# Cutting the w_up matmuls of a hybrid decoder layer into parts of other widths and column orders

## The chip, the cores and the metric

The kernel runs on one core of one Trainium2 chip. The metric is the device time of one execution in microseconds (us). A core has five engines that run side by side: PE (TensorE, matrix multiplication), DVE (VectorE), ACT (ScalarE), POOL (GpSimd) and SP (SyncE, which here only issues DMAs). The profile shows two rows for PE: PE is the streaming of a matmul's columns, PEld is the loading of its stationary operand, the "weights" of that one instruction, which may overlap the matmul before it.

## What is computed

One decoder layer over a sequence of 256 tokens with model width 2048. Attention comes first, and then the part that the change touches: a gated MLP whose up-projection is followed by a causal convolution of width 3 over time.

```python
D_MODEL = 2048
SEQ = 256
D_FF = 5632
...
        x = x + rmsnorm(mix, post_mix_g[l])
        h = rmsnorm(x, pre_ffn_g[l])
        u = causal_dwconv(h @ w_up[l], conv_w[l], conv_b[l])
        gate, val = jnp.split(u, 2, axis=-1)
        y = (jax.nn.gelu(gate, approximate=True) * val) @ w_down[l]
        x = x + rmsnorm(y, post_ffn_g[l])
```

All of it is float32. `w_up` is 2048 x 11264, so `h @ w_up` has 44 blocks of 256 output columns: 22 for the gate and 22 for the value.

## The kernel before

**Split numbers.** Every float32 operand of a large product is kept as two numbers, a rounded high part (type F32R) and the rest, a low part. A product is then high times high, plus low times high, plus high times low; the fourth, low times low, is left out. The activations of the MLP lie transposed in a tile `hT`, 128 partitions by 16 blocks `kt` by 512 columns: columns 0 to 255 of a block are the high parts of the 256 tokens, columns 256 to 511 the low parts.

**One projection.** `proj_T` computes one block of 256 output columns. It has two PSUM banks of 512 columns, one for each 128 output columns. `high(u)` (line 261) multiplies the high weights of four `kt` with all 512 columns of `hT`, so that a bank gets high x high in its left half and high x low in its right half. `low(u)` (line 268) multiplies the low weights with the 256 high columns and adds them into the right half. ACT later copies out the right half and DVE adds the left one to it (`conv`, lines 853 and 854). A projection of w_up has thus 32 matmuls of 512 columns (16 `kt` by 2 banks) and 32 of 256 columns, each with its own 128 x 128 block of weights:

```python
                    pe.matmul(b, hi[:, a, m * P:(m + 1) * P], hT[:, kt, 0:512], start=(kt == 0),
                              stop=(last == (0, kt)))
```

The runs `LONG = ((0, 1), (0, 1, 2, 3), (2, 3))` order them: two units of high, four of low and high as listed, 16 + 32 + 16 instructions of one kind each when seen from PE.

**The loop.** The MLP runs in two halves. A half does 11 groups `g`; each group has a gate projection and a value projection of 256 columns, with GELU, product and split into `G` behind them. Then the same half's rows of `w_down` are multiplied (`mm3`, line 283). The very first gate block is done by `first_gate` (lines 879 and 884). That leaves 43 calls of `proj_T` for w_up: 21 in the first half, 22 in the second. Banks alternate between two sets ("acc" and "att"), so that the evacuation of one projection runs beside the matmuls of the next.

**Who feeds PE.** SP loads weights in units of 128 x 1024 (line 71), ACT rounds them to the high part (`whi`, line 117), DVE subtracts to get the low part (`wlo`, line 120). Five buffers each hold `raw`, `whi` and `wlo`. The order of PE's instructions is that in which the program issues them; the order of ACT, DVE, POOL and SP within the MLP is set by a scheduler that plans with costs of its own. DMAs of weights go through SP's queue alone.

**Other matmuls** are used below as yardsticks: `mm3` on line 283 with 512, 384, 272 and 256 columns; the attention scores on line 449, where the two heads `e` of a pair use 64 of the 128 rows of the array each, with 256 and 128 columns of F32R; transposes (lines 484 and 732) of 128 plain float32 columns; and a reduction with a single column (line 651).

Of the kernel before, what the change touches and what calls it, by code (L numbers as in the profile page):

```python
# [17 lines left out]
P = 128  # L18
# [4 lines left out]
KT = D // P  # L23
# [3 lines left out]
HOLD = 6  # L27
LOW = (14, 4, 4, 4)
ROOM = 112


@with_exitstack
def hybrid_layer(ctx: ExitStack, tc: tile.TileContext, x, pre_mix_g, w_in, b_forget, sinks,
# [3 lines left out]
    pe, act, dve, pool, sp = nc.tensor, nc.scalar, nc.vector, nc.gpsimd, nc.sync  # L37
# [9 lines left out]

    small.tile([P, ROOM], F32, tag="room", bufs=1, name="room")
    ctx.enter_context(tc.manual_schedule(engines={mybir.EngineType.PE}))
# [7 lines left out]
    def tick():  # L57
        now[0] += 1
        for f in todo.pop(now[0], []):
            f()  # L60
# [8 lines left out]
    def w_load(src, a, c, pin=False):  # L69
        raw = wp.tile([P, UNIT], F32, tag="raw", bufs=5, name="raw")  # L70
        i = sp.dma_start(raw[:, :a * c].rearrange("p (a c) -> p a c", a=a), src)
        if pin:
            tc.keep_in_program_order(i)
        return raw, a, c
# [31 lines left out]
    def w_split(unit, pin=False, keep=None, begun=None, between=None,  # L106
                held=True):

        raw, a, c = unit
        n = a * c  # L110
        hi, lo = begun or w_parts(n, keep, held)
        for i in range(2 if between else 1):
            cs = slice(i * 512, i * 512 + 512) if between else slice(0, n)
            if i:
                between()
            if not between or i:
                i1 = act.copy(hi[:, cs], raw[:, cs])  # L117
                if pin:
                    tc.keep_in_program_order(i1)
            i2 = dve.tensor_tensor(lo[:, cs], raw[:, cs], hi[:, cs].bitcast(F32), op=ALU.subtract)  # L120
            if pin:
                tc.keep_in_program_order(i2)
        return [x.rearrange("p (a c) -> p a c", a=a) for x in (hi, lo)]

    def w_unit(src, a, c, keep=None):
        return w_split(w_load(src, a, c), keep=keep, held=False)

    def w_rows(w, k0, a, c0, c):
        return w[k0 * P:(k0 + a) * P, c0:c0 + c].rearrange("(a p) c -> p a c", p=P)
# [59 lines left out]
    hT = main.tile([P, KT, 512], F32R, tag="hT", name="hT")  # L189
# [27 lines left out]
    def unit_T(parts, u, banks, ticks=True, halves=False):  # L217
# [25 lines left out]
        if ticks:  # L243
            tick()

    def proj_T(w, c0, banks, runs=((0, 1), (0, 1), (2, 3), (2, 3))):

        parts, last = {}, ((len(runs) - 1) % 2, KT - 1)
        unit[0], period[0] = 0, 4 if len(runs) == 3 else 2

        def get(u):
            if u not in parts:
                parts[u] = w_split(w_load(w_rows(w, u * 4, 4, c0, 256), 4, 256))
            return parts[u]

        def high(u):
            hi = get(u)[0]
            for a in range(4):
                kt = u * 4 + a
                for m, b in enumerate(banks):  # L260
                    pe.matmul(b, hi[:, a, m * P:(m + 1) * P], hT[:, kt, 0:512], start=(kt == 0),  # L261
                              stop=(last == (0, kt)))

        def low(u):
            lo = get(u)[1]
            for a in range(4):
                for m, b in enumerate(banks):
                    pe.matmul(b[:, 256:512], lo[:, a, m * P:(m + 1) * P],  # L268
                              hT[:, u * 4 + a, 0:256], start=False,
                              stop=(last == (1, u * 4 + a)))  # L270

        for n, us in enumerate(runs):
            for u in us:
                (low if n % 2 else high)(u)
                tick()
# [13 lines left out]
    with tc.tile_pool(name="mixp", bufs=1) as mp:  # L289
# [311 lines left out]
        for p0, npair, cols in ((0, 3, 384), (3, 3, 384), (6, 2, 272)):  # L601
# [3 lines left out]
            for k0 in range(0, KT, per):  # L605
                na = min(per, KT - k0)
                hi, lo = w_unit(w_rows(w_in, k0, na, c0, cols), na, cols)
                for a in range(na):
                    kt = k0 + a
# [104 lines left out]
        hT = hT2  # L714
# [104 lines left out]
    with tc.tile_pool(name="ffn", bufs=1) as fp:  # L819
# [86 lines left out]
        for half in range(2):  # L906
# [47 lines left out]
            for n in range(3 + (half == 0)):  # L954
                b2 = [bank(), bank()]
                for u in range(FHALF // 2):
                    hi, lo = w_unit(w_rows(w_down, half * FHALF + u * 2, 2, n * 512, 512), 2, 512)
# [18 lines left out]
        def rstd_y(t, n, v):  # L976
            v2 = small.tile([P, 1], F32, tag="rv", name="rv")
            dve.tensor_tensor(v2, ysq[t][:, n:n + 1], v, op=ALU.add)
            r = small.tile([P, 1], F32, tag="ry", bufs=2, name="ry")
            pool.tensor_tensor(r, v2, mhalf, op=ALU.pow)  # L980
            return r
# [15 lines left out]
        for u in range(FHALF // 2):  # L997
            hi, lo = w_unit(w_rows(w_down, FHALF + u * 2, 2, 1536, 512), 2, 512,
                            keep=(None, [rest[:, c:c + 2, :].rearrange("p a c -> p (a c)")
                                         for c in (4 * (u - LAST), 4 * (u - LAST) + 2)])  # L1000
                            if LAST <= u < FHALF // 2 - 4 else None)
# [13 lines left out]
        r = rstd_y(0, 3, v)  # L1015
        for n in range(4):
            finish(0, slice(n * 512, (n + 1) * 512), r, sp)
        last = fp.tile([P, 256], F32, tag="last", name="last")
        for h in range(2):
# [5 lines left out]
            if h:  # L1025
                r = rstd_y(1, 4, v)
            gained(last if h else y_sb[:, 1, 1536:1792], b1[h], halves[h])
        for i, n in enumerate((512, 512, 512, 256, 256)):
            c = (0, 512, 1024, 1536, 1792)[i]
# [30 lines left out]
```

## Time and profile before

| | |
|---|---|
| median of 2 runs | 1066.99 us (1066.96 to 1067.03) |
| the profiled execution, its own time | 1067.17 us |
| its span, first to last instruction | 1065.3 us |
| PE busy | 1055.4 us, 99% of the span, 5974 matmuls |
| DVE, ACT, POOL busy | 738.3, 614.0, 226.2 us |
| granted TensorE clock | 0.998 |
| w_up, first half of the MLP | about 350.7 to 575.8 us |
| w_up, second half of the MLP | about 695.6 to 936.2 us |

A row of a timeline gives the start in us, the duration, the engine, the line, the operation, the names "out<-in", the shape and the number of like instructions that were merged into it. The shape of a matmul is "weights rows*columns", then "partitions x streamed columns". A matmul's recorded duration holds the way through the array as well, which overlaps the next matmul, so the cost of one in a stream is the distance from start to start; a merged row's start and the next row's start give it, divided by the count. A row "x from y [idle before <-releaser]" names what ended an idle time. The "windows" view gives busy time per engine in a stretch.

### The profile page before, as it was taken

What the parts mean: (1) busy time and instruction counts of PE and PEld (TensorE: products, weight loads), DVE (VectorE), ACT (ScalarE), POOL (GpSimd) and SP (SyncE); (2) the same over time, 40 slices, a digit from 0 to 9 for tenths busy, and PEclk for the clock granted to TensorE, in tenths of its full rate; (3) what the DMA queues carried; (4) which work ended last, traced back from release to release, by engine and by line L of the source; (5) the groups of instructions that cost most, each with busy time, mean ns of one, the idle gap of its engine ahead of it and who ended that gap; (6) DMA issues with size and microseconds to landing.
All of it is one profiled execution on the core that took longest, in us unless ns stands there. A gap on an engine that the chain in (4) does not pass through costs nothing.

```text
span 1065.3 us, 16215 instructions
## 1 busy us (share of the span) xinstructions
PE 1055.4 (99%) x5974; PEld 919.2 (86%) x5974; DVE 738.3 (69%) x1200; ACT 614.0 (58%) x1062; POOL 226.2 (21%) x250
## 2 busy tenths in 40 slices
PE   9999999999999999999999999999999999999997
PEld 7889988888889888888888888888888888888886
DVE  5989868886568877777677444457777777755563
ACT  6776757767548655556565443456565555644450
POOL 4353245440122312112121000002121212201110
PEclk9999999999999999999999999999999999999999
DMA  8645667545863766566666666666666666666642
GB/s 290 191 127 175 181 191 213 176 153 160 296 223 122 236 197 193 183 198 197 197 187 185 202 196 195 194 186 198 183 199 192 195 181 198 197 195 194 192 170 79
DMA packets 164970, 202.88 MB, mean 190 GB/s; under 512 B 6780, under 2 KB 130972, under 8 KB 164380
## 3 DMA queue, kind: packets, MB, share of 16 engines
q1 hardware_dynamic: 164572, 201.45, 61.2%
q8 instruction: 47, 0.77, 0.3%
q10 hardware_dynamic: 320, 0.40, 0.1%
q14 instruction: 31, 0.25, 0.1%
HBM read 199.58 MB, written 2.11 MB: 189 GB/s over the span
## 4 chain that ended last, share of the span: by engine, by line
PE 94%; DVE 2%; issue 1%; DMA 1%; ACT 1%; POOL 1%; SPq 0%; DVEq 0%; POOLq 0%; ACTq 0%
PE bank_acc L283 34%; PE bank_acc L261 22%; PE bank_att L261 14%; PE bank_acc L268 11%; PE bank_att L268 7%; PE bank_att L449 1%; PE bank_att L484 1%; PE bank_att L493 1%; DVE wlo L120 1%; PE bank_acc L879 1%; PE bank_att L283 1%; DMA x_in<-in_x_dram 1%; PE bank_att L495 0%; PE bank_att L732 0%; POOL scr L416 0%
## 5 line engine op out<-in xcount | busy, mean ns | idle before, releaser
L120 DVE TENSOR_TENSOR wlo<-raw,whi 128x1024 fp32r<-128x1024 f32 (+3 forms) x357 | 435.7, 1230 | 239.1 <-ACT whi L117 232.7
L117 ACT CAST whi<-raw 128x1024 fp32r<-128x1024 f32 (+3 forms) x356 | 363.3, 1035 | 269.2 <-issue 121.2
L261 PE MATMUL bank_acc<-hT,whi 128*128 128x512 f32 x1088 | 260.6, 391 | 0.0
L261 PEld LDWEIGHTS bank_acc<-hT,whi 128*128 128x128 f32 x1088 | 200.1, 188 | 39.5
L283 PE MATMUL bank_acc<-whi,G 128*128 128x512 f32 x652 | 202.7, 389 | 0.0
L855 POOL TENSOR_TENSOR u<-u,rowf 128x256 f32<-128x256 f32 x88 | 96.6, 1118 | 493.5 <-DVE u L854 490.6
L261 PE MATMUL bank_att<-hT,whi 128*128 128x512 f32 x640 | 150.6, 390 | 0.0
L283 PEld LDWEIGHTS bank_acc<-whi,G 128*128 128x128 f32 x652 | 122.4, 188 | 25.0
L261 PEld LDWEIGHTS bank_att<-hT,whi 128*128 128x128 f32 x640 | 118.7, 188 | 23.9
L268 PEld LDWEIGHTS bank_acc<-hT,wlo 128*128 128x128 f32 x1088 | 131.1, 188 | 3.3
L268 PE MATMUL bank_acc<-hT,wlo 128*128 128x256 f32 x1088 | 133.4, 278 | 0.0
L283 PE MATMUL bank_acc<-wlo,G 128*128 128x512 f32 x326 | 126.9, 389 | 0.0
L283 PE MATMUL bank_acc<-whi,oT 128*128 128x512 f32 (+1 forms) x272 | 81.7, 379 | 0.0
L268 PEld LDWEIGHTS bank_att<-hT,wlo 128*128 128x128 f32 x640 | 76.0, 188 | 1.7
L268 PE MATMUL bank_att<-hT,wlo 128*128 128x256 f32 x640 | 76.3, 277 | 0.0
L283 PEld LDWEIGHTS bank_acc<-wlo,G 128*128 128x128 f32 x326 | 61.2, 188 | 12.3
L283 PEld LDWEIGHTS bank_acc<-whi,oT 128*128 128x128 f32 x272 | 50.2, 188 | 9.3
L283 PE MATMUL bank_acc<-wlo,oT 128*128 128x512 f32 (+1 forms) x136 | 51.2, 377 | 0.0
L283 PE MATMUL bank_acc<-whi,hT 128*128 128x384 f32 (+1 forms) x192 | 46.9, 323 | 0.0
L857 ACT ACTIVATE yg<-u,cw 128x256 f32<-128x256 f32 x44 | 26.5, 602 | 27.5 <-POOL u L855 27.5
L857 ACT ACTIVATE yv<-u,cw 128x256 f32<-128x256 f32 x44 | 26.4, 603 | 26.5 <-POOL u L855 26.5
L416 POOL TENSOR_TENSOR scr<-scr 128x256 f32<-128x256 f32 x26 | 26.7, 1042 | 57.2 <-DVE scr L415 34.3
(212 smaller groups left out, 1056.5 us busy)
## 6 DMA issues: line engine op xcount, KB each, us to landing
raw<-in_w_up_dram SPq DMA_DIRECT2D x176, 512.0 KB, 4.1
raw<-in_w_down_dram SPq DMA_DIRECT2D x88, 512.0 KB, 4.7
raw<-in_w_in_dram SPq DMA_DIRECT2D x51, 512.0 KB, 4.7
raw<-in_w_out_dram SPq DMA_DIRECT2D x32, 512.0 KB, 4.7
raw<-in_w_in_dram SPq DMA_DIRECT2D x16, 384.0 KB, 3.3
cb<-c_dram SPq DMA_DIRECT2D x8, 256.0 KB, 4.3
x_sb<-in_x_dram SPq DMA_DIRECT2D x2, 1024.0 KB, 5.9
raw<-in_w_in_dram SPq DMA_DIRECT2D x5, 408.0 KB, 4.1
```

Source lines behind the costliest of these rows:

```text
L117: i1 = act.copy(hi[:, cs], raw[:, cs])
L120: i2 = dve.tensor_tensor(lo[:, cs], raw[:, cs], hi[:, cs].bitcast(F32), op=ALU.subtract)
L261: pe.matmul(b, hi[:, a, m * P:(m + 1) * P], hT[:, kt, 0:512], start=(kt == 0), stop=(last == (0, kt)))
L268: pe.matmul(b[:, 256:512], lo[:, a, m * P:(m + 1) * P], hT[:, u * 4 + a, 0:256], start=False, stop=(last == (1, u * 4 + a)))
L283: pe.matmul(b, a, r[:, cols], start=(first and i == 0), stop=(last and i == 2))
L416: pool.tensor_tensor(dst, dst, row, op=ALU.mult)
L449: pe.matmul(sb[e][:, cs], a[r, t * P:(t + 1) * P], b[r, 0:nk], start=(n == 0), stop=(n == 2))
L484: pe.transpose(pb[:, i * P:(i + 1) * P], p[:, e, c:c + P], ident)
L493: pe.matmul(ov, values(hl, 0), p[:, :, 0:256], start=(n == 0), stop=False)
L855: pool.tensor_tensor(u[:, 2:258], u[:, 2:258], rowf, op=ALU.mult)
L857: act.activation(y, u[:, 2:258], AF.Identity, bias=cw[:, 3, ch:ch + 1], scale=cw[:, 2, ch:ch + 1])
L879: pe.matmul(v(b, t), gate[kt][0][:, ms], v(hT[:, kt, 0:512], t), start=(t == 0 and kt == 0), stop=False)
```

## The change

A table gives one form to every two of the 43 projections (`cut_no // 2 % 21`; forms 0 and 20 cut nothing, and the 43rd projection has form 0 again). `WIDE` applies to the 512-column matmuls, except those of the first and the last `kt`, so to 28 of the 32 of a projection; `NARROW` applies to all 32 of 256 columns. A tuple is a list of widths: the matmul becomes that many matmuls, each with a slice of the columns of `hT` and of the bank, and with the same weights. A negative number `-q` leaves one matmul, but its columns are read and written in another order: q columns of the left half, q of the right half, the next q of the left half, and so on.

```diff
+WIDE = (
+    (), (256, 256), (128, 128, 128, 128), (384, 128), (128, 384), (320, 192), (448, 64),
+    (128, 256, 128), (240, 272), (256, 128, 128), (272, 240), -128, -64, -16, -2, (), (), (), (), (),
+    (),
+)
+NARROW = (
+    (), (), (), (), (), (), (), (), (), (), (), (), (), (), (), (128, 128), (192, 64), (144, 112),
+    (160, 96), -16, (),
+)
+
+
+def cut_up(form, a, n):
+
+    if not form:
+        return [a]
+    if isinstance(form, int):
+        return [a.rearrange("p (h c q) -> p c h q", h=2, q=-form)]
+    at = [sum(form[:i]) for i in range(len(form) + 1)]
+    return [a[:, i:j] for i, j in zip(at, at[1:])]
...
+    cut_no = [0]
+
     def proj_T(w, c0, banks, runs=((0, 1), (0, 1), (2, 3), (2, 3))):
...
+        wide = narrow = ()
+        if len(runs) == 3:
+            wide, narrow = WIDE[cut_no[0] // 2 % 21], NARROW[cut_no[0] // 2 % 21]
+            cut_no[0] += 1
...
-                    pe.matmul(b, hi[:, a, m * P:(m + 1) * P], hT[:, kt, 0:512], start=(kt == 0),
-                              stop=(last == (0, kt)))
+                    form = () if kt in (0, KT - 1) else wide
+                    for o, r in zip(cut_up(form, b, 512), cut_up(form, hT[:, kt, 0:512], 512)):
+                        pe.matmul(o, hi[:, a, m * P:(m + 1) * P], r, start=(kt == 0),
+                                  stop=(last == (0, kt)))
...
-                    pe.matmul(b[:, 256:512], lo[:, a, m * P:(m + 1) * P],
-                              hT[:, u * 4 + a, 0:256], start=False,
-                              stop=(last == (1, u * 4 + a)))
+                    for o, r in zip(cut_up(narrow, b[:, 256:512], 256),
+                                    cut_up(narrow, hT[:, u * 4 + a, 0:256], 256)):
+                        pe.matmul(o, lo[:, a, m * P:(m + 1) * P], r, start=False,
+                                  stop=(last == (1, u * 4 + a)))
```

In the changed kernel lines 261 and 268 are 288 and 297. On PE in the first half, where forms 1 and 2 begin, the rows (line, operation, out<-in, partitions x columns, count; `hT_3640` is the activation tile, `whi` and `wlo` the weights' high and low parts) read before:

```order
L261 MATMUL bank_acc<-hT_3640,whi 128x512 x16
L268 MATMUL bank_acc<-hT_3640,wlo 128x256 x32
L261 MATMUL bank_acc<-hT_3640,whi 128x512 x32
L268 MATMUL bank_acc<-hT_3640,wlo 128x256 x32
L261 MATMUL bank_acc<-hT_3640,whi 128x512 x16
```

and after:

```order
L288 MATMUL bank_acc<-hT_3640,whi 128x512 x2
L288 MATMUL bank_acc<-hT_3640,whi 128x256 x28
L297 MATMUL bank_acc<-hT_3640,wlo 128x256 x32
L288 MATMUL bank_acc<-hT_3640,whi 128x256 x28
L288 MATMUL bank_acc<-hT_3640,whi 128x512 x4
L288 MATMUL bank_acc<-hT_3640,whi 128x128 x56
L297 MATMUL bank_acc<-hT_3640,wlo 128x256 x32
```

Nothing changes place; 14 matmuls of 512 columns on either side of the low ones have become 28 of 256 in one projection and 56 of 128 in the next. On PE in the second half, where the last interleaved form (runs of two columns) is followed by the first cut of the low matmuls, it reads after:

```order
L288 MATMUL bank_acc<-hT_3640,whi 128x128x2x2 x14
L297 MATMUL bank_acc<-hT_3640,wlo 128x256 x32
L288 MATMUL bank_acc<-hT_3640,whi 128x128x2x2 x14
L288 MATMUL bank_acc<-hT_3640,whi 128x512 x18
L297 MATMUL bank_acc<-hT_3640,wlo 128x128 x64
L288 MATMUL bank_acc<-hT_3640,whi 128x512 x16
```

There the interleaved matmul is still one instruction of 512 columns, and 32 low ones have become 64. On DVE in the first half, from the third group on, the scheduler sets one subtraction of weights (`wlo`) behind the split of `G`, the product of gate and value. Before:

```order
L930 TENSOR_TENSOR yv<-yv,yg 128x256 x2
L120 TENSOR_TENSOR wlo<-raw,whi 128x1024
L287 TENSOR_TENSOR G_3959<-yv,G_3959 128x256
L287 TENSOR_TENSOR G_3960<-yv,G_3960 128x256
L120 TENSOR_TENSOR wlo<-raw,whi 128x1024 x2
```

After:

```order
L958 TENSOR_TENSOR yv<-yv,yg 128x256 x2
L315 TENSOR_TENSOR G_3959<-yv,G_3959 128x256
L315 TENSOR_TENSOR G_3960<-yv,G_3960 128x256
L139 TENSOR_TENSOR wlo<-raw,whi 128x1024 x3
```

The subtraction moves behind two short instructions. ACT's roundings (`whi`) move in the same way, by one or two places, about the two GELU instructions of a group. POOL and SP keep their order.

## The prediction

> **What bounds the kernel now.** I read the page first, then the windows over the two w_up stretches, then what PE waited for.
>
> ```profile
> PE 1055.4 (99%) x5974; PEld 919.2 (86%) x5974; DVE 738.3 (69%) x1200; ACT 614.0 (58%) x1062; POOL 226.2 (21%) x250
> ```
> ```profile
> 350.66:575.80 225.14, 225.14 (x1323) 198.97 (x1322) 168.55 (x250) 132.34 (x207) 46.53 (x42) 1.00 0.64 196
> 695.62:936.20 240.58, 240.58 (x1409) 212.49 (x1408) 174.80 (x254) 138.61 (x216) 46.61 (x42) 1.00 0.63 192
> ```
> ```profile
> PE bank_acc L172 <- DVE junk L167: 1.3, 1, 1.3
> PE bank_att L493 <- DVE pl L287: 0.4, 1, 0.4
> ```
>
> The windows' columns are length, then busy time of PE, PEld, DVE, ACT and POOL with counts, granted clock, DMA share, GB/s. In both w_up stretches PE is busy for all of the time at clock 1.00, DVE for 73 to 75% of it, ACT for 58 to 59%, the DMA engines for 63 to 64%. PE's two waits in the whole run lie at lines 172 and 493, outside w_up. So the time of w_up is the sum of the distances between matmul starts; whatever a cut matmul costs more is added to the span one for one. Each of the 5974 matmuls has a weight load of its own.
>
> The present distances, from one projection:
>
> ```profile
> 702.90 7.45 PE L261 MATMUL bank_acc<-hT,whi 128*128 128x512 f32 x32
> 710.19 3.82 PE L268 MATMUL bank_acc<-hT,wlo 128*128 128x256 f32 x32
> 713.85 0.63 PE L261 MATMUL bank_acc<-hT,whi 128*128 128x512 f32 x2
> ```
>
> 32 of 512 columns take 710.19 - 702.90 = 7.29 us, 0.2278 each; 32 of 256 take 3.66 us, 0.1144 each.
>
> **What a part of another width costs.** For 384 and 272 columns line 283 has rows (seven and six groups of three matmuls between the rows shown); for 256 lines 879 and 884:
>
> ```profile
> 84.79 0.51 PE L283 MATMUL bank_acc<-whi,hT 128*128 128x384 f32 x2
> ...
> 88.43 0.51 PE L283 MATMUL bank_acc<-whi,hT 128*128 128x384 f32 x2
> ...
> 122.17 0.41 PE L283 MATMUL bank_acc<-whi,hT 128*128 128x272 f32 x2
> ...
> 124.42 0.41 PE L283 MATMUL bank_acc<-whi,hT 128*128 128x272 f32 x2
> ```
> ```profile
> 331.62 4.00 PE L879 MATMUL bank_acc<-hT,whi 128*128 128x256 f32 x32
> 335.46 2.43 PE L732 MATMUL bank_att<-ident,x_sb 128*128 128x128 f32 x16
> ...
> 338.01 2.02 PE L884 MATMUL bank_acc<-hT,wlo 128*128 128x256 f32 x16
> 339.87 0.88 PE L879 MATMUL bank_acc<-hT,whi 128*128 128x256 f32 x6
> ```
>
> That is 3.64 / 21 = 0.173 us for 384 and 2.25 / 18 = 0.125 for 272. From 384 to 512 a column costs 0.0545 / 128 = 0.00043, which leaves a fixed share of about 0.010. Between the rows: 320 columns 0.146, 448 columns 0.200. 256 columns take 0.120 on line 879, 0.116 on line 884, 0.114 on line 268; for high weights I take 0.118.
>
> Below 256 the line would go on falling (64 columns: 0.04), if the weight load did not hold it up. Two places show the load:
>
> ```profile
> 157.99 0.64 PEld L651 LDWEIGHTS bank_att<-ones,sqs 128*128 128x128 f32 x4
> 158.55 0.54 PEld L268 LDWEIGHTS bank_acc<-hT,wlo 128*128 128x128 f32 x4
> ```
> ```profile
> 158.22 0.50 PE L651 MATMUL bank_att<-ones,sqs 128*128 128x1 f32 x4
> ```
> ```profile
> 244.86 0.28 PE L449 MATMUL bank_att<-keys,ql 64*128 64x128 f32 x2
> 244.97 0.28 PE L449 MATMUL bank_att<-keys,qh 64*128 64x128 f32 x2
> 245.19 0.50 PE L283 MATMUL bank_acc<-whi,oT 128*128 128x512 f32 x1
> 245.53 0.39 PE L283 MATMUL bank_acc<-wlo,oT 128*128 128x512 f32 x1
> ```
> ```profile
> 244.81 0.20 PEld L449 LDWEIGHTS bank_att<-keys,ql 64*128 64x128 f32 x2
> 244.92 0.20 PEld L449 LDWEIGHTS bank_att<-keys,qh 64*128 64x128 f32 x2
> 245.19 0.19 PEld L283 LDWEIGHTS bank_acc<-whi,oT 128*128 128x128 f32 x1
> 245.29 0.19 PEld L283 LDWEIGHTS bank_acc<-wlo,oT 128*128 128x128 f32 x1
> 245.53 0.41 PEld L283 LDWEIGHTS bank_acc<-whi,oT 128*128 128x128 f32 x2
> ```
>
> Four matmuls of a single column start at 158.22, and the load after theirs starts at 158.55: 0.33 us for three loads, 0.11 each, with next to nothing streamed. The 128-column scores, two row halves at a time, stand 0.11 apart, and so do their loads. At 245.19 a 512-column matmul starts together with its load: it lasts 0.50 instead of 0.39 and the next starts 0.34 later instead of 0.228, so a load that nothing covers adds 0.11. The load after it begins at 245.29, when the first is done, and the third at 245.53, when the second matmul starts: there is room for one load ahead, no more. So a matmul costs the larger of its stream and one load: **0.113 us for every part of 240 columns or fewer**, the middle of 0.109 (three loads in 0.33) and 0.120 (the dearest 256-column row, which may be load or stream).
>
> **The sum.** 28 cut matmuls by 2 projections are 56 per wide form; 32 by 2 are 64 per narrow form. Against 0.2278 us, in ns per cut matmul:
> - (256, 256): 2 x 118, +8. (240, 272) and (272, 240): 113 + 125, +10 each.
> - 4 x 128: 4 x 113 = 452, +224.
> - (384, 128) and (128, 384): 173 + 113, +58 each.
> - (320, 192): 146 + 113, +31. (448, 64): 200 + 113, +86.
> - (128, 256, 128) and (256, 128, 128): 118 + 226, +116 each.
> - the four interleaved forms: 0, see below.
>
> Together 717 ns x 56 = 40.2 us. Each of the four narrow cuts makes 113 + 113 of 114.4, +112 whatever the two widths are; 4 x 112 x 64 = 28.6 us. In all +68.8 us: 40 in the first half, 29 in the second.
>
> The interleaved forms have no row with runs this short. Nearest is line 879, whose 256 columns come in two runs of 128, read and written: 0.120 against 0.116 for line 884 without a break, and against 0.114 to 0.120 over all unbroken rows of 256. So 128-column runs are within 0.004 us of free, and I put 0 for all. If one break cost 0.004, runs of 2 (255 breaks) would cost 1 us per matmul; half the rate instead, as the transposes below show, +0.21. I keep +12 us (56 x 0.21, the runs of 2 alone) for the range.
>
> Costed at nothing: the 1040 further instructions' issue (loads and matmuls of single columns are taken every 0.11 us above, parts come no faster); the evacuation on ACT and DVE, the weights' preparation and the DMAs, which have 25 to 42% of w_up to spare and get more, since PE's stretch grows and their work doesn't; and the `wlo` that moves behind two DVE splits of G:
>
> ```profile
> L120 DVE TENSOR_TENSOR wlo<-raw,whi 128x1024 fp32r<-128x1024 f32 x84 | 103.0, 1237 | 47.6 <-ACT whi L117 47.6
> L287 DVE TENSOR_TENSOR G<-yv,G 128x256 fp32r<-128x256 f32 x20 | 7.6, 421 | 0.0
> ```
>
> That makes it 0.84 us later. A unit (8 high and 8 low matmuls) holds PE for 2.74 us, there are five buffers of prepared weights, and this DVE work idles 47.6 us for want of `whi` in the stretch, so a delay of 0.84 us is made up before PE comes to it. If that cover were gone, each group would lose up to 0.84 us, 20 x 0.84 = 17 us, and PE would show waits for `wlo`. ACT's shift of one or two places is covered in the same way.
>
> The profiled execution took 1067.17 us, 1.9 more than its span; 1067.2 + 68.8 = **1136 us**. The median is 0.2 us below that execution, which changes nothing.
>
> **A rule of the Trainium skill, weighed.** The Trainium skill, "TensorE: Matmul & The Clock Gate", section "Back-to-back issue gap", gives about 81 ns per pair of load and matmul at 128 columns. By it the 1296 parts under 256 columns would be 0.032 us cheaper and the sum 41 us smaller, 1095 us. The trace disagrees with it for these operands: its 128-column pairs stand 0.11 us apart.
>
> **Rivals.**
>
> *The parts share a load* (not slower). If a second matmul with the same weights skipped its load, an extra part would cost only the fixed 0.010 us: 1040 x 0.010 = 10 us, 1078 us, 1% over before. For it: all parts of a cut have the same weights. Against it: in `mm3` two matmuls in a row have the same G as weights, and each has its load:
>
> ```profile
> L283 PE MATMUL bank_acc<-wlo,G 128*128 128x512 f32 x326 | 126.9, 389 | 0.0
> L283 PEld LDWEIGHTS bank_acc<-wlo,G 128*128 128x128 f32 x326 | 61.2, 188 | 12.3
> ```
>
> It decides once PE shows clearly fewer loads than matmuls. Chance 0.07.
>
> *Under 256 columns F32R streams at half the rate*, as float32 transposes do:
>
> ```profile
> L484 PE MATMUL bank_att<-ident,p 128*128 128x128 f32 x96 | 13.1, 272 | 0.0
> ```
> ```profile
> 257.94 0.82 PE L484 MATMUL bank_att<-ident,p 128*128 128x128 f32 x6
> ```
> ```profile
> 42.93 0.22 PE L449 MATMUL bank_att<-keys,qh 64*128 64x128 f32 x1
> 42.99 0.27 PE L449 MATMUL bank_att<-keys,ql 64*128 64x128 f32 x1
> ```
>
> Six transposes of 128 columns span 0.82 us and one lasts 0.27, so they start 0.11 apart, 0.00085 per column. Then 240 columns cost 0.204, 192 cost 0.164, 160 and 144 cost 0.136 and 0.123, narrower ones 0.113 still; the sums become 53 and 34 us, 1154 us. Against it stand the last two rows: in the second row half of a score, 128 columns of F32R are followed by the next matmul after 0.06 us (its load was early). Chance 0.06.
>
> *Broken column orders are slow.* All interleaved matmuls at half the rate: 4 x 56 x 0.21 + 64 x 0.104 = 54 us more, 1190 us. The Trainium skill, "PSUM — Partial Sum Buffer", section "Specifications (TRN2)", says that any non-contiguous access pattern in PSUM slows matmuls significantly; line 879 above, broken once, shows at most 0.004 us of it. Chance 0.07; that only runs of 2 suffer (1148 us), 0.09.
>
> That the change doesn't cut is no rival: the rows of the changed program show each part.
>
> **How the numbers follow.** The load floor with free interleaving, 0.66, gives 1136 us. Its bounds: a floor of 0.109 and 0.114 for 256 give 1296 x 0.004 + 224 x 0.004 = 6 us less, 1130; a floor of 0.120 gives 9 us more, 1145. With the runs of 2 (1148) and the half rate (1154, with its own 4 us of floor) the range of 1128 to 1160 holds 0.8. Outside lie the shared load, the broad slowdown, and 0.05 for anything else, such as a throttled clock while PE streams little. A difference under 2% is about what cannot be told from no change. Only the shared load ends within it: faster 0.01, same 0.07, slower 0.92.
>
> **What would show it.** PE and PEld both near 7014 instructions. In the first half the stretch of w_up 40 us longer, in the second 29. The 4 x 128 form: 0.113 from start to start, loads without gaps. The four narrow cuts all alike; (320, 192) cheaper than (384, 128) and that cheaper than (448, 64), because only the columns taken from the wide part save time. The interleaved forms at 0.228. Wrong it would be if narrow parts of different widths cost different times, if loads go missing, if 16- or 2-column runs stand out, or if PE waits for `wlo` or `whi`.

## The result, and the profile after

| | |
|---|---|
| median of 2 runs, after | 1143.95 us (1143.91 to 1144.00) |
| median of 2 runs, before | 1066.99 us |
| ratio after to before, with 95% interval | 1.072 [1.068, 1.077], slower |
| span of the profiled execution, after | 1142.1 us (+76.8) |

The first line of the page after, busy time, share of the span and instructions of each engine:

```profile
PE 1131.8 (99%) x7014; PEld 1010.6 (88%) x7014; DVE 739.7 (65%) x1200; ACT 617.0 (54%) x1062; POOL 209.9 (18%) x250
```

All that PE waited for in the whole execution after, in us, times and longest:

```profile
PE bank_acc L191 <- DVE junk L186: 1.3, 1, 1.3
PE bank_att L521 <- DVE pl L315: 0.4, 1, 0.4
```

The two stretches of w_up after (columns as in the windows of the prediction):

```profile
345.03:616.56 271.53, 271.53 (x2110) 264.84 (x2109) 174.42 (x258) 138.24 (x213) 34.56 (x44) 1.00 0.55 169
736.27:1012.54 276.27, 276.27 (x1694) 243.00 (x1692) 176.12 (x254) 138.90 (x217) 44.81 (x42) 1.00 0.55 168
```

PE grew by 76.4 us and by exactly 1040 matmuls and 1040 loads; the other engines have as many instructions as before. PE still never stands in w_up, its clock is 1.00, and DVE, ACT and the DMAs have a smaller share of a longer stretch than before. The same two stretches before, from the first matmul of w_up to the first one behind it:

```profile
345.35:575.94 230.59, 230.59 (x1355) 203.73 (x1353) 173.45 (x258) 135.60 (x213) 48.07 (x44) 1.00 0.65 198
695.62:936.30 240.68, 240.68 (x1410) 212.55 (x1408) 174.90 (x254) 138.64 (x217) 46.61 (x42) 1.00 0.63 192
```

They grew by 40.9 and 35.6 us, together 76.5 of the 76.8 us of added span. The forecast had 40 and 29.

Where in w_up it went, PE's timeline shows. From the start of the low matmuls (line 297) of one projection to those of the next of the same form is one whole projection. Without a cut it takes 721.13 - 710.19 = 10.94 us, as two rows of the kernel before show:

```profile
710.19 3.82 PE L268 MATMUL bank_acc<-hT,wlo 128*128 128x256 f32 x32
...
721.13 3.81 PE L268 MATMUL bank_att<-hT,wlo 128*128 128x256 f32 x32
```

First half, two rows each of the forms (256, 256), 4 x 128, (384, 128), (320, 192) and (448, 64):

```profile
371.54 3.84 PE L297 MATMUL bank_att<-hT,wlo 128*128 128x256 f32 x32
...
382.85 3.84 PE L297 MATMUL bank_acc<-hT,wlo 128*128 128x256 f32 x32
...
397.02 3.98 PE L297 MATMUL bank_acc<-hT,wlo 128*128 128x256 f32 x32
...
414.21 3.88 PE L297 MATMUL bank_att<-hT,wlo 128*128 128x256 f32 x32
...
429.08 3.88 PE L297 MATMUL bank_att<-hT,wlo 128*128 128x256 f32 x32
...
441.70 3.98 PE L297 MATMUL bank_acc<-hT,wlo 128*128 128x256 f32 x32
...
479.34 3.95 PE L297 MATMUL bank_att<-hT,wlo 128*128 128x256 f32 x32
...
491.27 3.87 PE L297 MATMUL bank_acc<-hT,wlo 128*128 128x256 f32 x32
...
503.83 4.01 PE L297 MATMUL bank_acc<-hT,wlo 128*128 128x256 f32 x32
...
517.30 4.01 PE L297 MATMUL bank_att<-hT,wlo 128*128 128x256 f32 x32
```

Second half, two rows each of the interleaved forms with runs of 128, 16 and 2 columns, and of the narrow cuts (128, 128), (192, 64) and (160, 96):

```profile
751.26 3.82 PE L297 MATMUL bank_acc<-hT,wlo 128*128 128x256 f32 x32
...
762.20 3.82 PE L297 MATMUL bank_att<-hT,wlo 128*128 128x256 f32 x32
...
795.20 3.83 PE L297 MATMUL bank_acc<-hT,wlo 128*128 128x256 f32 x32
...
806.51 3.83 PE L297 MATMUL bank_att<-hT,wlo 128*128 128x256 f32 x32
...
819.10 3.83 PE L297 MATMUL bank_att<-hT,wlo 128*128 128x256 f32 x32
...
833.12 3.83 PE L297 MATMUL bank_acc<-hT,wlo 128*128 128x256 f32 x32
...
845.66 7.26 PE L297 MATMUL bank_acc<-hT,wlo 128*128 128x128 f32 x64
...
860.08 7.26 PE L297 MATMUL bank_att<-hT,wlo 128*128 128x128 f32 x64
...
874.50 7.23 PE L297 MATMUL bank_att<-hT,wlo 128*128 128x192 f32 x64
...
888.93 7.23 PE L297 MATMUL bank_acc<-hT,wlo 128*128 128x192 f32 x64
...
932.23 7.24 PE L297 MATMUL bank_att<-hT,wlo 128*128 128x160 f32 x64
...
946.67 7.24 PE L297 MATMUL bank_acc<-hT,wlo 128*128 128x160 f32 x64
```

Each distance less 10.94, divided by the 28 (wide) or 32 (narrow) cut matmuls of a projection, is what one cut matmul cost more. Forms without rows above are read from the same timeline in the same way.

| form | one projection, us | more per cut matmul, ns | forecast, ns |
|---|---|---|---|
| (256, 256) | 11.31 | 13 | 8 |
| 4 x 128 | 17.19 | 223 | 224 |
| (384, 128); (128, 384) | 12.62; 12.64 | 60; 61 | 58 |
| (320, 192) | 11.93 | 35 | 31 |
| (448, 64) | 13.47 | 90 | 86 |
| (128, 256, 128); (256, 128, 128) | 14.14; 14.23 | 114; 118 | 116 |
| (240, 272); (272, 240) | 11.28; 11.27 | 12 | 10 |
| runs of 128; of 64 | 10.94; 10.94 | 0 | 0 |
| runs of 16 | 11.31 | 13 | 0 |
| runs of 2 | 14.02 | **110** | **0** |
| all four narrow cuts | 14.42 to 14.44 | 109 | 112 |
| low matmuls, runs of 16 | 11.13 | 6 | 0 |

Two projections each, the wide cuts make 41.4 us (forecast 40.2), the narrow cuts 27.9 (28.6), the interleaved forms 7.3 (0): 76.6 us of the 76.8. So the whole of the result lies in these rows; of the 8 us that were missing in the forecast 7.3 lie in the interleaved forms, 6.2 of them in the runs of 2. All of the interleaved forms stand in the second half, which is the one that outgrew its forecast.

### The profile page after: what moved, and what is told of

Same layout as the page of the kernel before. It is cut to its first block, busy times and chain, and to the rows that moved or that the text cites. A ratio compares the mean times of both kernels' runs of the same rounds, so it can differ in the third digit from the quotient of the medians.

```text
span 1142.1 us, 18299 instructions
## 1 busy us (share of the span) xinstructions
PE 1131.8 (99%) x7014; PEld 1010.6 (88%) x7014; DVE 739.7 (65%) x1200; ACT 617.0 (54%) x1062; POOL 209.9 (18%) x250
## 4 chain that ended last, share of the span: by engine, by line
PE 96%; DVE 2%; issue 1%; DMA 0%; ACT 0%; POOL 0%; DVEq 0%; POOLq 0%; SPq 0%; ACTq 0%
PE bank_acc L311 31%; PE bank_acc L288 23%; PE bank_att L288 15%; PE bank_acc L297 12%; PE bank_att L297 8%; PE bank_att L477 1%; PE bank_att L512 1%; PE bank_att L521 1%; PE bank_acc L907 1%; PE bank_acc L243 1%; PE bank_att L311 1%; PE bank_att L243 1%; DVE wlo L139 0%; PE bank_att L523 0%; PE bank_att L760 0%
## 5 line engine op out<-in xcount | busy, mean ns | idle before, releaser
L139 DVE TENSOR_TENSOR wlo<-raw,whi 128x1024 fp32r<-128x1024 f32 (+3 forms) x357 | 440.6, 1245 | 311.7 <-ACT whi L136 289.5
L288 PE MATMUL bank_acc<-hT,whi 128*128 128x512 f32 (+7 forms) x1508 | 284.4, 344 | 0.0
L288 PEld LDWEIGHTS bank_acc<-hT,whi 128*128 128x128 f32 x1508 | 233.9, 189 | 31.6 <-issue 0.3
L883 POOL TENSOR_TENSOR u<-u,rowf 128x256 f32<-128x256 f32 x88 | 81.3, 946 | 585.4 <-DVE u L882 582.4
L288 PE MATMUL bank_att<-hT,whi 128*128 128x512 f32 (+6 forms) x1004 | 173.8, 331 | 0.0
L288 PEld LDWEIGHTS bank_att<-hT,whi 128*128 128x128 f32 x1004 | 149.4, 190 | 17.9 <-issue 0.2
L297 PE MATMUL bank_acc<-hT,wlo 128*128 128x256 f32 (+4 forms) x1216 | 148.4, 278 | 0.0
L297 PEld LDWEIGHTS bank_acc<-hT,wlo 128*128 128x128 f32 x1216 | 145.2, 189 | 2.6
L297 PEld LDWEIGHTS bank_att<-hT,wlo 128*128 128x128 f32 x768 | 90.1, 189 | 1.2
L297 PE MATMUL bank_att<-hT,wlo 128*128 128x256 f32 (+7 forms) x768 | 91.0, 277 | 0.0
```

The lines of the kernel that those rows point to most:

```text
L288: pe.matmul(o, hi[:, a, m * P:(m + 1) * P], r, start=(kt == 0), stop=(last == (0, kt)))
L297: pe.matmul(o, lo[:, a, m * P:(m + 1) * P], r, start=False, stop=(last == (1, u * 4 + a)))
L883: pool.tensor_tensor(u[:, 2:258], u[:, 2:258], rowf, op=ALU.mult)
```

## The experiments

**e1: the short runs put back.** Does the excess over the forecast lie in the interleaving alone?

```diff
-    (128, 256, 128), (240, 272), (256, 128, 128), (272, 240), -128, -64, -16, -2, (), (), (), (), (),
+    (128, 256, 128), (240, 272), (256, 128, 128), (272, 240), -128, -64, (), (), (), (), (), (), (),
...
-    (160, 96), -16, (),
+    (160, 96), (), (),
```

> The changed kernel with its three costly interleaved forms (runs of 2 and of 16 columns in the 512-column matmuls, runs of 16 in the 256-column ones) put back to one unbroken run; nothing is left out. Theory (the 8 us over the forecast are the short runs): in the changed kernel's trace a projection with runs of 2 takes 14.01 us, with runs of 16 11.30, with low runs of 16 11.13, an uncut one 10.94, so two projections each give back 2 x (3.07 + 0.36 + 0.19) = 7.2 us: about 1136.7 us. Rival (the excess is spread over the cuts, and the interleaved projections are slow for another reason, such as their neighbours or their place): under 2 us back, above 1142.

Measured 1137.15 us (1136.97 to 1137.45), ratio to before 1.065 [1.064, 1.067]: 6.8 us below the changed kernel, where the rows above give 7.3. What is left, 1137.15, is 1.2 us above the forecast, which had priced these forms at nothing. Most of the miss lies in them.

**e2: fewer columns of weights.** Is the floor of 0.11 us the load of the weights, or a fixed time of any narrow matmul? Forms now name the widths and the number M of weight columns that are used.

```diff
-                        pe.matmul(o, hi[:, a, m * P:(m + 1) * P], r, start=(kt == 0),
+                        pe.matmul(o[0:M], hi[:, a, m * P:m * P + M], r, start=(kt == 0),
```

> Cut matmuls whose weights have 128, 64 or 32 columns instead of 128; with 64 or 32 the outputs of the other weight columns are left out, so the result is not the layer's. Form by form, per uncut matmul of 512 columns: theory (a part costs the larger of its stream and one weight load, and a load takes 0.11 us per 128 weight columns): 4 x 128 with 128 weights 0.443 us; with 64 weights the load is 0.055, about as long as the stream of 128 columns, so 0.23 to 0.26; with 32 the same 0.23 to 0.24. 8 x 64 with 128 weights 0.89; with 64 weights 0.45; with 32 weights 0.24 to 0.27. (384, 128) with 64 weights 0.24 instead of 0.285, (448, 64) 0.26 instead of 0.307. Low matmuls: 2 x 128 with 64 weights 0.12 to 0.13 instead of 0.222, 4 x 64 with 128 weights 0.444, with 64 0.225. Rival (a narrow F32R matmul has a time of its own of 0.11, whatever is loaded): 0.44 and 0.89 at every number of weights.

Six windows of e2, each a half projection: 56 quarters with M = 128, M = 64 and M = 32, then 112 eighths with M = 128, M = 64 and M = 32, each with two unbroken matmuls:

```profile
385.30:391.96 6.66, 6.66 (x59) 6.57 (x58) 5.36 (x11) 4.26 (x8) 1.23 (x2) 1.00 0.50 159
409.94:413.82 3.88, 3.88 (x60) 3.79 (x59) 1.66 (x2) 1.08 (x2) 0.00 (x0) 1.00 0.65 188
432.97:436.84 3.87, 3.87 (x60) 3.79 (x58) 1.68 (x2) 1.08 (x2) 0.00 (x0) 1.00 0.60 181
494.24:518.84 24.60, 24.60 (x115) 24.41 (x114) 5.27 (x11) 4.28 (x8) 1.23 (x2) 0.50 0.07 21
570.33:577.28 6.95, 6.95 (x115) 6.82 (x114) 5.35 (x11) 4.43 (x8) 1.23 (x2) 1.00 0.51 153
600.21:604.26 4.05, 4.05 (x116) 3.88 (x114) 3.57 (x7) 2.74 (x5) 1.24 (x2) 1.00 0.51 155
```

Less 2 x 0.228 us, a quarter takes 6.20 / 56 = 0.111 us with 128 weight columns and 0.061 with 64 and with 32; an eighth takes 6.49 / 112 = 0.058 with 64 and 3.59 / 112 = 0.032 with 32. An eighth with 128 weight columns, where the clock is full (single starts from 449 us on), takes 0.112. So with the same 64 streamed columns the time halves from 128 to 64 weight columns, and the floor of 0.11 is the load; a fixed time for a narrow matmul falls. The quarter that stays at 0.061 when its weights are halved once more is then held by the stream of its 128 columns. Whether the 0.032 is the load of 32 weight columns or the stream of 64, these runs don't tell. The Trainium skill, "TensorE: Matmul & The Clock Gate", section "LDWEIGHTS (loading the stationary operand)", gives columns / 1.2 ns, that is 107 and 53 for 128 and 64 columns; these runs lie 4 to 5 ns above each.

The fourth row was not expected: PE is busy all the time, yet the granted clock is 0.50. An uncut matmul takes 0.427 us there by single starts, so an eighth with full weights takes (24.60 - 2 x 0.427) / 112 = 0.21 us. See e6.

**e3: only the read, or only the write.** Matmuls of the interleaved forms read `hT` in SBUF and write a bank of PSUM in the broken order. Here one of the two stays plain ("=") and the other is broken ("-": runs in turns from the two halves; "s": every other run, then the rest).

```diff
+    if how == "-":
+        return a.rearrange("p (h c q) -> p c h q", h=2, q=q)
+    if how == "s":
+        return a.rearrange("p (c h q) -> p h c q", h=2, q=q)
+    return a.rearrange("p (c h q) -> p c h q", h=2, q=q)
...
+                    pe.matmul(cut_up(form, b, 1), hi[:, a, m * P:(m + 1) * P],
+                              cut_up(form, hT[:, kt, 0:512], 0), start=(kt == 0),
```

> One matmul of 512 columns each, whose columns are read in broken order and written in plain order, or read plain and written broken, or both, with runs of 1, 2, 4, 8, 16, 32 columns; breaks jump between the halves (256 columns away) or skip one run (short jump). Where reading and writing differ, columns land in other places, so the result is not the layer's. In the changed kernel runs of 2 on both sides cost 0.336 us, of 16 0.240, of 64 and 128 0.228 like unbroken ones. Theory W (the write into PSUM pays for each short run): written broken alone 0.33 (runs of 2) and 0.24 (16), read broken alone 0.228. Theory R (the read of SBUF pays): the reverse. Theory S (both pay, and they add): each alone about half, 0.28 and 0.234. Both broken, by one column's time (0.42 ns) per run: runs of 1 0.44, of 4 0.28, of 8 0.255, of 32 0.235; by whole lines instead, runs of 32 are free and 4 and 8 lie between. If the distance of the jump matters, short jumps are cheaper; if only the break counts, the same.

PE's timeline of e3: the first two rows are one projection with only the read in runs of 2, the other two one with only the write in runs of 2:

```profile
373.36 3.85 PE L296 MATMUL bank_att<-hT,wlo 128*128 128x256 f32 x32
...
387.40 3.84 PE L296 MATMUL bank_acc<-hT,wlo 128*128 128x256 f32 x32
...
399.94 3.82 PE L296 MATMUL bank_acc<-hT,wlo 128*128 128x256 f32 x32
...
410.88 3.82 PE L296 MATMUL bank_att<-hT,wlo 128*128 128x256 f32 x32
```

14.04 us against 10.94: the read pays all of it, (14.04 - 10.94) / 28 = 0.111 us, and the write nothing at all. By the median distances of single starts, in ns: only the read in runs of 2, 337, and of 16, 240; read and write in runs of 4, 8 and 32, 251, 243 and 237; only the read in every other run of 2, 451. Every form that only writes in runs of 2 or 16, near or skipped, takes 228, as the plain one does. The same holds for the 256 columns of the low matmuls (read in runs of 2: 166, written so: 114). The rule of the Trainium skill that the prediction weighed ("PSUM — Partial Sum Buffer", section "Specifications (TRN2)"), of any non-contiguous pattern in PSUM, isn't borne out for these writes. Writes in single columns were not tried.

**e4: where the high weights begin.** Does the fixed share of some 0.010 us that the prediction read out of the wide matmuls come from an unlucky place of weights and activations to each other? The kernel before, with the high weights begun 0 to 64 columns further on; an unused tile shrinks from 112 to 32 columns to make space.

```diff
+SHIFT = (0, 4, 8, 12, 16, 20, 24, 28, 32, 36, 40, 44, 48, 52, 56, 60, 64, 1, 2, 6, 0)
...
+        hi = where.tile([P, UNIT + 64 * (where is wp)], F32R, tag=pre + "hi", bufs=nb, name="whi")
...
+            hi = hi[:, shift[0]:]
```

> The kernel before, uncut, with the high weights of every two projections begun 0 to 64 columns (4 bytes each) further on in a buffer wider by 64 columns; the whole layer is computed. A 512-column matmul takes 0.227 us where its columns alone would take 0.213 at the slope of the widths, and low matmuls, which are already placed at chosen offsets, show 0.113 to 0.120. Theory (the extra 0.013 comes from where weights and columns lie relative to each other): some shifts give 0.220 or less, others 0.227 to 0.235, and the projections' times differ by up to 0.2 us and more. Rival (it is a fixed cost of a matmul): all shifts give 0.226 to 0.228.

1076.40 us in one run, against 1067.33 for the kernel before on the same chip. By single starts, shifts of 0, 60 and 64 give 228 ns, 48 gives 229, 2, 6 and 44 give 230, the others 232 to 234; none is faster. So the place matters, but only upwards, and the fixed share is not explained by it.

**e5: which reads are slow.** Writes plain, reads as in e3 with more runs, and unbroken reads begun some columns on.

```diff
+    if form[0] == "+":
+        return x.rearrange("p k c -> p (k c)")[:, kt * 512 + form[1]:kt * 512 + form[1] + n]
+    if form[0] == "-":
+        return x[:, kt, 0:n].rearrange("p (h c q) -> p c h q", h=form[1], q=form[2])
+    return x[:, kt, 0:n].rearrange("p (c h q) -> p h c q", h=form[1], q=form[2])
```

> Writes in plain order throughout; only the order or the place in which a matmul reads its columns differs, so columns land in other places and the result is not the layer's. Shapes: two halves interleaved in single columns; two passes that take every other run of 4, 8, 32, 64 columns; four quarters interleaved in runs of 2, 16, 64; unbroken reads that begin 2, 4, 8, 16, 32, 64, 128 columns further on. So far per 512 columns, reads broken alone: 0.337 us for runs of 2 from two halves, 0.451 for every other run of 2, 0.251 for 4, 0.243 for 8, 0.240 for 16, 0.237 for 32, 0.228 for 64 and unbroken. Theory (each run shorter than some 64 columns costs by the lines of SBUF that it touches, whatever the distance): every other run of 4, 8, 32 like the halves, 0.25, 0.243, 0.237; of 64 free; quarters in runs of 16 and 64 like halves, 0.240 and 0.228, in runs of 2 above 0.337 or like the skipped runs, 0.451; single columns 0.45 or more. Rival (distance or direction matters: what is near costs more): every other run of 4 or 8 above 0.26. Unbroken reads that begin elsewhere: theory 0.227 from every place, rival (the 0.013 over the columns' own time comes from the place) some below 0.222.

Median distances of single starts, in ns: every other run of 4, 233; of 8, 232; of 32, 236; of 64, 228. Runs from the four quarters in turns: of 2, 444; of 16, 232; of 64, 228. Unbroken, begun 2, 4, 8, 16 or 32 columns on: 230 to 233; 64 or 128 on: 228. So 64 columns in a row are free, and a start off a multiple of 64 costs 2 to 5 ns. Every other run of 4 or 8 costs less than such runs from the two halves (251 and 243 in e3), so neither the theory nor the rival on distance holds. One form went the other way: **single columns, taken in turns from the two halves, 215.8 on a mean**, less than the unbroken read. PE's timeline of e5, one projection with it:

```profile
371.52 3.84 PE L290 MATMUL bank_att<-hT,wlo 128*128 128x256 f32 x32
...
382.17 3.84 PE L290 MATMUL bank_acc<-hT,wlo 128*128 128x256 f32 x32
```

10.65 us against 10.94 with 28 of the 64 matmuls changed. The Trainium skill, "TensorE: Matmul & The Clock Gate", section "Back-to-back issue gap", has N / 2.4 + 2.5 ns for an isolated matmul, 215.8 at 512 columns: the reads in turns come out at that, the unbroken ones 12 ns above it. So 12 ns of an unbroken 512-column matmul, about as much as the fixed share that e4 looked for, are a matter of the read.

**e6: when the clock falls.** The changed kernel with thinner parts: A is 4 x 112 and 64, B is 5 x 96 and 32, C is 6 x 80 and 32, E is 8 x 64.

```diff
+A, B, C, E = (112,) * 4 + (64,), (96,) * 5 + (32,), (80,) * 6 + (32,), (64,) * 8
+WIDE = ((), A, (), B, (), C, (), E, (), A, (), B, (), (128,) * 4, (), (), (), (), (), (), ())
```

> Uncut projections alternate with cut ones: 512 columns in 5 parts (112 x 4, 64), 6 parts (96 x 5, 32), 7 parts (80 x 6, 32) and 8 parts (64 x 8), then 5 and 6 parts together with the low matmuls in 2 and 3 parts, 4 x 128 with 2 x 128, 3 low parts alone and 4 x 64 low parts alone; the whole layer is computed. Per cut matmul at full clock the load floor gives 0.56, 0.67, 0.78 and 0.89 us, low ones 0.222, 0.335, 0.446. In the run with fewer weights 8 x 64 fell to a granted clock of 0.5 after 4 us and then took 1.71. Theory (the clock is granted by how much PE streams, and falls when the columns' share of the time is under some third): 8 x 64 (share 0.24) and 4 x 64 low lose the clock in part, 5 parts (0.38) keep it, 6 and 7 parts (0.32, 0.27) lie at the edge; with the low matmuls cut as well nothing recovers in between, and 6 parts lose more. Rival (the clock falls only with 64-column parts, or by the number of instructions): 5, 6 and 7 parts all at full clock and the floor.

1484.42 us, mean clock 0.866. Three windows of e6: two half projections with five parts; a half projection with six parts, the second in a row; and 32 low matmuls alone in three parts of 96, 96 and 64:

```profile
379.99:396.46 16.47, 16.47 (x146) 16.30 (x145) 6.58 (x12) 5.51 (x9) 1.23 (x2) 1.00 0.41 128
...
463.28:481.91 18.63, 18.63 (x88) 18.43 (x86) 5.27 (x11) 4.28 (x8) 1.24 (x2) 0.50 0.10 29
...
1144.13:1159.34 15.21, 15.21 (x97) 15.21 (x96) 3.74 (x6) 2.88 (x5) 0.00 (x0) 0.68 0.36 109
```

Five parts take (16.47 - 4 x 0.228) / 28 = 0.556 us and keep the clock, also with halved low matmuls beside them; six take 0.670 where the clock is still full, by single starts, and lose it: (18.63 - 2 x 0.427) / 14 = 1.27 in the second row. PE and its loads are busy in both, so busy time is not what keeps the clock. What differs is how many columns are streamed: 512 / 0.556 = 920 per us keeps it, 512 / 0.670 = 764 per us does not, and neither do the low matmuls of the third row, 256 / 0.335 = 764 per us without a part of 32 columns; the eighths of e2 fit on either side, 512 / 0.894 = 573 per us with M = 128 (lost) and 512 / 0.467 = 1096 with M = 64 (kept). Seven and eight parts, and low matmuls alone in four parts, lose it too. The thinnest form of the change, 4 x 128, streams 512 / 0.443 = 1156 per us; with the low matmuls halved beside it, it keeps the clock here.

**e7, e8, e10: reading in turns on purpose.** e7 is the kernel before with the 256 tokens of `hT` stored so that the read takes one column from each half in turn and still meets the tokens in order; PSUM is written plainly. e8 does the same to the streamed weights of 512 columns in `mm3`, e10 also to those of 384 and 272 columns; ACT and DVE, which split them, store them so.

```diff
+    return a.rearrange("p (h c) -> p c h", h=2)
...
-                    pe.matmul(b, hi[:, a, m * P:(m + 1) * P], hT[:, kt, 0:512], start=(kt == 0),
+                    pe.matmul(b, hi[:, a, m * P:(m + 1) * P], by_turns(r) if turned else r,
...
-                    act.activation(hT[:, kt, t * P:(t + 1) * P], b, AF.Copy,
+                    act.activation(places(kt, 0, t), apart(b), AF.Copy,
```

> The kernel before, uncut, with the activations of w_up stored by even and odd tokens: the even columns of the logical 512 in the first half of a block, the odd ones in the second, written so by ACT and DVE, and read by every w_up matmul in turns, one column from each half; PSUM is written in plain order, and the whole layer is computed. In the run with read orders 512 columns read in turns took 0.216 us where unbroken ones took 0.2278. Theory (the read of SBUF costs the 0.012 us, and turns avoid it): 43 x 32 matmuls save 0.012 each, 16.5 us, the 256-column ones nothing (a load holds them at 0.111 to 0.114): 1050 us. Rival (0.216 held only because the columns landed elsewhere or the weights' buffers lay well): 1064 to 1070; if ACT and DVE pay for the scattered writes on the path between attention and MLP, up to 3 us less gain.

> As the run before it, and the 512-column units of w_out and w_down, which are streamed against stationary activations, are rounded and subtracted into the same order of even and odd columns (ACT and DVE read the raw weights with a step of two) and read in turns. Theory: 1014 w_down and some 380 w_out matmuls of 512 columns save 0.0115 us each, 16 us more than the run before: about 1034 us. Rival (a step of two makes ACT's 1.05 us or DVE's 1.23 us per unit longer): if a unit of 12 matmuls, 2.7 us of PE, still covers both, no loss; if DVE takes twice as long, 2.5 us, PE starts to wait for the weights and the gain of the second part goes.

> As the run with w_up and the 512-column weights read in turns, and also the streamed weights of the value projection, 384 and 272 columns, stored by even and odd columns and read in turns; the whole layer is computed. Theory: 192 matmuls of 384 and 96 of 272 columns save 0.010 us each, 2.9 us: 1028.4 us. Rival (half a width of 192 or 136 columns is no distance that helps, or DVE's longer subtraction is waited for there): 1031 or more.

| | median, us | ratio to before | verdict at 2% |
|---|---|---|---|
| e7 | 1046.71 (1046.57 to 1047.03) | 0.981 [0.979, 0.983] | unclear |
| e8 | 1031.30 (1031.13 to 1031.82) | 0.967 [0.965, 0.968] | faster |
| e10 | 1029.06 (1028.84 to 1029.14) | 0.964 [0.963, 0.966] | faster |

e7's change is a shade under the 2% from which a verdict calls it faster, but it is far above the spread of the runs, under 0.5 us. e7 gained 20.4 us, more than was put down for it. A projection takes 10.48 us in it, 43 x 0.46 = 19.8 us less, and 0.08 of the 0.46 come from the low matmuls (32 in 3.57 us instead of 3.65). e8 gained another 15.4 us (16 expected) and e10 another 2.2 (2.9 expected). In e8 the cost moved to the engines that store the weights: ACT's rounding of a unit of 512-column weights rose from 1050 to 1559 ns and DVE's subtraction from 1249 to 1541, and none of PE's waits is for them. e10, page and one projection of the timeline with both kinds of matmul read in turns:

```profile
PE 1015.6 (99%) x5974; PEld 913.3 (89%) x5974; DVE 775.2 (75%) x1200; ACT 676.4 (66%) x1062; POOL 230.3 (22%) x250
```
```profile
698.30 3.73 PE L297 MATMUL bank_att<-hT,wlo 128*128 128x256 f32 x32
...
708.78 3.73 PE L297 MATMUL bank_att<-hT,wlo 128*128 128x256 f32 x32
```

PE has the 5974 matmuls of the kernel before and 39.8 us less work; a projection takes 10.48 us. e10 is faster than both kernels of this case.

**e9: how many places, how far apart.** Writes plain, single columns in turns from h equal pieces; a negative number -g takes them from the two halves of each of g pieces.

```diff
+    if form < 0:
+        return a.rearrange("p (g h c) -> p g c h", h=2, g=-form)
+    return a.rearrange("p (h c) -> p c h", h=form)
```

> Reads in turns of single columns from 2, 4, 8, 16, 32, 64, 128 or 256 equal pieces of the 512 columns (so the next column lies 256, 128, 64, 32, 16, 8, 4 or 2 columns on), then in turns from the two halves of each half, quarter, sixteenth and 64th; low matmuls from 2 to 128 pieces of 256. Writes stay in plain order, so columns land in other places and the result is not the layer's. So far: two halves 0.216 us, unbroken 0.228, runs of 2 from two halves 0.337. Theory (two columns in a row from one short line of SBUF wait on each other, columns from different places don't): all distances down to about 16 columns give 0.216, and short ones (2, 4, 8 columns) become slow. Rival (only some distances do, those that fall into another part of the memory): some of the distances 16 to 256 give 0.216, others 0.228 or more.

PE's timeline of e9, one projection each with two places, with four, with eight, and with two places only 4 columns apart:

```profile
371.55 3.84 PE L287 MATMUL bank_att<-hT,wlo 128*128 128x256 f32 x32
...
382.19 3.84 PE L287 MATMUL bank_acc<-hT,wlo 128*128 128x256 f32 x32
...
393.78 3.83 PE L287 MATMUL bank_acc<-hT,wlo 128*128 128x256 f32 x32
...
406.25 3.94 PE L287 MATMUL bank_att<-hT,wlo 128*128 128x256 f32 x32
...
421.75 3.87 PE L287 MATMUL bank_att<-hT,wlo 128*128 128x256 f32 x32
...
440.16 3.87 PE L287 MATMUL bank_acc<-hT,wlo 128*128 128x256 f32 x32
...
808.40 3.82 PE L287 MATMUL bank_att<-hT,wlo 128*128 128x256 f32 x32
...
819.02 3.82 PE L287 MATMUL bank_acc<-hT,wlo 128*128 128x256 f32 x32
```

10.64, 12.47, 18.41 and 10.62 us. By single starts: two places 216 ns at every distance tried (4, 16, 64, 128 and 256 columns), four places 282, eight 490, sixteen to 256 places 430 to 459. The number of places counts and, for two places, the distance doesn't; neither theory, as it was put down, had both.

## Why the prediction was right, and where a term was off

The forecast was 1136 us with a range of 1128 to 1160, and 1143.95 was measured. The floor by the load and the sum over the forms held; one of the prediction's own signs of being wrong, that runs of 16 or 2 stand out, came all the same, because the interleaved forms had been put at nothing. Step by step:

- *PE bounds w_up, and a dearer matmul adds itself to the span one for one.* It did: +76.8 us of span, +76.6 us summed over the forms, no wait of PE in w_up before or after.
- *Every part has a load of its own, and below 240 columns the load is the cost.* 7014 matmuls and 7014 loads; the four narrow cuts cost +109 ns, all alike, whether 128 and 128 or 192 and 64. e2 shows that the load sets this. The floor is 0.111 us and the forecast had 0.113: -0.7 us over the narrow cuts.
- *Only the columns taken from the wide part save time.* (320, 192) came out at +35, (384, 128) at +60, (448, 64) at +90 ns, in the order and near the sizes forecast. The forms of about halves were forecast at +8 and +10 and cost +13 and +12: 256 columns of high weights take 0.120 rather than 0.118, and 272 columns some 0.128 rather than 0.125. The wide cuts came out 1.2 us dearer and the narrow ones 0.7 us cheaper than forecast, which cancels in part.
- A small share of the wide cuts isn't theirs. In the first half the uncut low matmuls beside them start 116.8 ns apart on a mean, 114.3 before, 1.7 us over 672 of them; the 32 at 397.02 last 3.98 us, those at 751.26, beside matmuls that cost nothing more, 3.82. e4 and e5 show steps of this size when the place of weights or activations changes. Whether a place is the cause here was not tried.
- *Interleaved forms at 0.* This is the term that was mis-sized: +7.3 us, of which runs of 2 are 6.2 and runs of 16 are 1.1 (wide and low). It rested on one row, line 879, whose runs are 128 columns long; that such runs are free was right (0 ns, and 0 for runs of 64), but nothing in it spoke of short ones. The prediction had a bound of +0.21 us per matmul for runs of 2; it is +0.110. The cost is in reading SBUF (e3). Runs of 64 are free, runs of 4 to 32 cost 4 to 23 ns of 228, runs of 2 cost 109 or more (e3, e5).
- *Costed at nothing* (issue, evacuation, preparation of weights, the `wlo` behind two splits): nothing of it shows. PE never waits for `wlo` or `whi`, and 1040 more instructions came at the loads' pace.
- The rivals: shared loads fall by the count of loads. Half rate below 256 columns falls by the narrow cuts, which would have cost different times; e2 has quarters at 0.061 us with few weights. That rival took its rate from transposes that start 0.11 apart; 0.11 is the floor by the load as well, so those rows did not show a rate. That all broken orders are slow falls by the runs of 64 and 128; that only runs of 2 suffer was the rival nearest to what came, with half its price and a little for runs of 16. So for these forms the mechanism was not foreseen; the range had 12 us for runs of 2, and the 7.3 us fell within that. The throttled clock that the prediction named as a remainder did not come here (1.00), but e6 has it 1.5 times further on: 764 columns per us against 1156.

## What to carry to other kernels

Where each matmul loads its own weights, its cost here was the larger of its stream and its load, 0.111 us for 128 weight columns; parts with 128 x 128 weights that stream fewer than about 240 columns all cost the same, and the way to cheaper narrow parts is fewer weight columns, not fewer streamed ones. The order in which a bank of PSUM is written cost nothing here, down to runs of 2 columns; the order in which SBUF is read did: keep 64 or more columns in a row, or read single columns from just two places in turn, which was faster than reading straight on for these 512-column F32R matmuls. A row that shows one break to be free says nothing of many breaks: price a pattern by its run length, and if no row has that length, keep the whole distance between the bounds as a term.

## What was not expected of the hardware

- A 512-column read in turns of single columns from two places takes 216 ns, unbroken 228; runs of two columns from the same two places take 337, and four places 282. The same runs of 2, every other one, take 451. Why two places help and four don't was not settled: e9 excludes distance as the reason.
- The granted clock fell to 0.50 while PE was busy without a gap, when it streamed 764 columns per us or fewer; at 920 it stayed at 1.00.
- An unbroken read begun 2 to 32 columns off costs 2 to 5 ns of 228, and high weights moved by 1 to 56 columns cost 1 to 6.
